# Softmax over rows of 1024: a hand-made critical section handed to the tile framework under a fixed schedule

## The chip, the cores and the metric

The kernel runs on one core of one Trainium2 chip. The metric is the device time of one execution in microseconds (us), the median of several runs.

## The reference, cut to what matters

```python
x: 32 x 512 x 1024 float32, temperature = 0.5
scaled  = x / temperature
shifted = scaled - max(scaled, axis=-1)
out     = exp(shifted) / sum(exp(shifted), axis=-1)
```

That is 16,384 rows of 1024 numbers. 67.11 MB are read and 67.11 MB written.

## The kernel before

The rows are cut into 16 tiles of 4 MB (128 partitions, 8 rows each). SyncE issues the loads, VectorE takes maxima and divides, ScalarE computes exponentials with their sums and issues the stores. Six places of 32 KB per partition form a ring: load i+6 waits until store i has landed. Every tile is worked on in two groups of four rows. All waits are written by hand, inside one critical section, with 37 semaphores: one for each load, one for each store, and five counters.

```python
LOADS = [8] * 16; STORES = [[8]] * 16; RING = 48; GROUP = 4
ring = pool.tile([P, RING, d], f32, name="ring")          # one tensor, six places
...
loaded = [tc.alloc_semaphore(f"loaded{i}") for i in range(len(LOADS))]
stored = [tc.alloc_semaphore(f"stored{i}") for i in range(len(parts))]
topped, biased, summed, inverted, scaled = (tc.alloc_semaphore(name) for name in ...)

def exponential(g):
    i, s, r, k = groups[g]
    nc.scalar.wait_ge(biased, g + 1)
    for a in range(k):
        ins = nc.scalar.activation(ring[:, s + a, :], ring[:, s + a, :], Exp,
              bias=bias[:, r + a : r + a + 1], scale=scale, accum_out=sums[:, r + a : r + a + 1])
    ins.then_inc(summed, 1)

def store(n):
    l, s, r, k = parts[n]
    nc.scalar.wait_ge(scaled, part_end[n])                 # the division of this tile only
    nc.scalar.dma_start(out=dram(of, r, k, l), in_=ring[:, s : s + k, :]).then_inc(stored[n], 16)

with tc.tile_critical():
    for i in range(len(LOADS)):
        load(i)                                            # from load 6 on: waits for stored[i - 6]
    for b in range(free_to + 1, len(parts)):
        nc.sync.wait_ge(stored[b], 16)
    ...                                                    # exponential(g), store(n) on ScalarE
    ...                                                    # maximum, shift, invert, divide on VectorE
```

Of the kernel before, what the change touches and what calls it, by code (L numbers as in the profile page):

```python
# [1 line left out]

# [4 lines left out]



LOADS = [8] * 16  # L10

STORES = [[8]] * 16

RING = 48

GROUP = 4


def _places(loads, ring):
    places, p = [], 0  # L20
    for k in loads:
        if p + k > ring:
            p = 0
        places.append(p)
        p += k
    return places


@with_exitstack
def kernel(  # L30
    ctx: ExitStack,
    tc: tile.TileContext,
    x: bass.AP,
    temperature: bass.AP,
    out: bass.AP,
):
    nc = tc.nc
    f32 = mybir.dt.float32
    scale = 1.0 / float(temperature)
    extreme = mybir.AluOpType.max if scale > 0 else mybir.AluOpType.min  # L40

    P = 128
    xf = x.flatten_outer_dims()
    of = out.flatten_outer_dims()
    n, d = xf.shape
    assert sum(LOADS) * P == n

    places = _places(LOADS, RING)
    first = [sum(LOADS[:i]) for i in range(len(LOADS))]
    total = sum(LOADS)  # L50

    pool = ctx.enter_context(tc.tile_pool(name="data", bufs=1))
    ring = pool.tile([P, RING, d], f32, name="ring")
    top = pool.tile([P, total], f32, name="top")
    bias = pool.tile([P, total], f32, name="bias")
    sums = pool.tile([P, total], f32, name="sums")
    recip = pool.tile([P, total], f32, name="recip")


    parts = []  # L60
    for i, ks in enumerate(STORES):
        j = 0
        for k in ks:
            parts.append((i, places[i] + j, first[i] + j, k))
            j += k
        assert j == LOADS[i]

    groups, part_end = [], []
    for i, s, r, k in parts:
        for a in range(0, k, GROUP):  # L70
            groups.append((i, s + a, r + a, min(GROUP, k - a)))
        part_end.append(len(groups))

    loaded = [tc.alloc_semaphore(f"loaded{i}") for i in range(len(LOADS))]
    stored = [tc.alloc_semaphore(f"stored{i}") for i in range(len(parts))]
    topped, biased, summed, inverted, scaled = (
        tc.alloc_semaphore(name)
        for name in ("topped", "biased", "summed", "inverted", "scaled")
    )

    def dram(t, r, k, i):

        block = t[P * first[i] : P * (first[i] + LOADS[i]), :]
        block = block.rearrange("(p k) d -> p k d", p=P, k=LOADS[i])
        return block[:, r - first[i] : r - first[i] + k, :]

    def maximum(g):
        i, s, r, k = groups[g]
        if g == 0 or groups[g - 1][0] != i:
            nc.vector.wait_ge(loaded[i], 16)  # L90
        nc.vector.tensor_reduce(  # L91
            out=top[:, r : r + k],
            in_=ring[:, s : s + k, :],
            axis=mybir.AxisListType.X,
            op=extreme,
        ).then_inc(topped, 1)

    def shift(g):
        i, s, r, k = groups[g]
        nc.vector.wait_ge(topped, g + 1)  # L100
        nc.vector.tensor_scalar_mul(  # L101
            bias[:, r : r + k], in0=top[:, r : r + k], scalar1=-scale
        ).then_inc(biased, 1)

    def exponential(g):
        i, s, r, k = groups[g]
        nc.scalar.wait_ge(biased, g + 1)
        for a in range(k):
            ins = nc.scalar.activation(  # L109
                ring[:, s + a, :],  # L110
                ring[:, s + a, :],
                mybir.ActivationFunctionType.Exp,
                bias=bias[:, r + a : r + a + 1],
                scale=scale,
                accum_out=sums[:, r + a : r + a + 1],
            )
        ins.then_inc(summed, 1)

    def invert(g):
        i, s, r, k = groups[g]  # L120
        nc.vector.wait_ge(summed, g + 1)
        nc.vector.reciprocal(recip[:, r : r + k], sums[:, r : r + k]).then_inc(inverted, 1)  # L122

    def divide(g):
        i, s, r, k = groups[g]
        nc.vector.wait_ge(inverted, g + 1)
        for a in range(k):
            ins = nc.vector.tensor_scalar_mul(  # L128
                ring[:, s + a, :], in0=ring[:, s + a, :], scalar1=recip[:, r + a : r + a + 1]
            )  # L130
        ins.then_inc(scaled, 1)

    def load(i):
        nonlocal free_to
        s, r, k = places[i], first[i], LOADS[i]

        for n, (l, s1, r1, k1) in enumerate(parts):
            if l < i and s1 < s + k and s < s1 + k1 and n > free_to:
                for b in range(free_to + 1, n + 1):
                    nc.sync.wait_ge(stored[b], 16)  # L140
                free_to = n
        nc.sync.dma_start(out=ring[:, s : s + k, :], in_=dram(xf, r, k, i)).then_inc(
            loaded[i], 16
        )

    def store(n):
        l, s, r, k = parts[n]
        nc.scalar.wait_ge(scaled, part_end[n])
        nc.scalar.dma_start(out=dram(of, r, k, l), in_=ring[:, s : s + k, :]).then_inc(
            stored[n], 16  # L150
        )

    free_to = -1
    with tc.tile_critical():  # L154
        for i in range(len(LOADS)):
            load(i)
        for b in range(free_to + 1, len(parts)):
            nc.sync.wait_ge(stored[b], 16)


        for g in range(len(groups) + 1):
            if g < len(groups):
                exponential(g)
            for n in range(len(parts)):
                if part_end[n] == g:
                    store(n)


        for g in range(len(groups) + 1):
            if g < len(groups):  # L170
                maximum(g)
                shift(g)
            if g > 0:
                invert(g - 1)
                divide(g - 1)


# [1 line left out]
_INS = ['x', 'temperature']  # L179
_OUTS = [((32, 512, 1024), 'float32')]  # L180

_NUMBERS = {'temperature': 0.5}


# [26 lines left out]
```

## Time and profile before

| | before |
|---|---|
| time, median of 6 runs | 318.76 us (318.69 to 318.99) |
| span in the profile | 317.0 us |
| bytes moved | 134.25 MB |
| VectorE, ScalarE busy | 74%, 47% |
| first load issued | 0.94 us |
| last store issued, landed | 302.64, 315.12 us |

Where a landing is given as a point of time, it is the end of the transfer's last packet, unless the text says otherwise. The semaphore that tells of it moves 0.3 to 0.4 us later (at 315.50 us for this store); the profile's times from issue to landing, and all waits, count to that.

First the page of the profile. The rows DMA and GB/s cut the span into 40 equal slices: the busy share of the 16 transfer engines in tenths, and what they moved.

```profile
span 317.0 us, 568 instructions
...
DVE 235.5 (74%) x224; ACT 149.6 (47%) x257; POOL 0.2 (0%) x4
...
DMA  8999999999999999999999999999999999999995
GB/s 323 405 459 409 389 442 418 447 428 442 434 430 438 422 438 426 442 422 442 422 447 430 434 434 430 435 426 438 430 438 435 434 426 434 434 426 434 430 434 232
```

No compute engine is full, but the transfers are, in every slice but the first and last. So the transfers bound the kernel. A load or a store of 4 MB that has the engines to itself takes up 9.68 us of them, which is 433 GB/s (the first three loads land at 13.02, 22.70 and 32.38 us; stores 12 to 14, after the last load, land 9.66 and 9.67 us apart), and the 32 of them come to 309.8 us. Loads and stores together move 432 to 435 GB/s in every stretch between 60 and 300 us.

Next the costliest groups (instruction, shapes, count, busy us, mean ns of one; after the last bar the idle time before it and what ended it) and the transfers (count, KB, median us from issue to landing).

```profile
L109 ACT ACTIVATE ring<-ring,bias 128x1024 f32<-128x1024 f32 x128 | 145.4, 1137 | 149.1 <-DVE bias L101 149.1
L91 DVE TENSOR_REDUCE top<-ring 128x4 f32<-128x4096 f32 x32 | 141.3, 4415 | 62.9 <-DMA ring<-in_x_dram 62.9
...
L109 ACT ACT_TABLE_LOAD x1 | 1.3, 1283 | 0.9 <-SPq L154 0.9
...
ring<-in_x_dram SPq DMA_DIRECT2D x16, 4096.0 KB, 49.9
out_dram<-ring ACTq DMA_DIRECT2D x16, 4096.0 KB, 38.9
```

ScalarE and VectorE have idle time to spare. The time from a store's issue to its landing, 38.9 us, is twice the 19.35 us between two stores; by the times to landing (38.9 and 49.9 us over 19.35) about two stores and two or three loads are under way at any time.

Last, the two ends: first the opening of the chain of waits (start us, length us, what), then the sequencers' instructions of the line that opens and closes the section (count, duration in ns as least/median/most, first and last start); those of the closing line follow in "More of the kernel before".

```profile
0.73 0.06 issue
0.78 0.03 SPq L206
0.82 0.12 issue
0.94 12.41 DMA ring<-in_x_dram
```

```profile
L154 SPq NOP  x2: 13/13/13, 0.7 to 316.0; - x2
L154 SPq EVENT_SEMAPHORE  x2: 17/22/28, 315.7 to 315.9; - x2
L154 SPq COMPARE_BRANCH  x1: 33/33/33, 315.6 to 315.6; - x1
L154 ACTq DRAIN  x1: 8/8/8, 315.8 to 315.8; - x1
L154 DVEq DRAIN  x1: 17/17/17, 315.8 to 315.8; - x1
...
```

```profile
L206 POOLq DRAIN  x3: 34/41/110, 0.7 to 316.7; - x3
...
L206 SPq COMPARE_BRANCH  x1: 33/33/33, 0.8 to 0.8; - x1
L206 POOLq EVENT_SEMAPHORE_RANGE_CLEAR  x1: 265/265/265, 316.4 to 316.4; - x1
```

The reader should see that a section costs a signal and a branch on the way in (0.7 to 0.9 us, before the first load), and a branch, a signal and drains on the way out (315.6 to 316.0 us, after the last store).

### The profile page before, as it was taken

The numbers are of one execution on the slowest core, as the hardware profiler recorded it, in microseconds if no ns is written. First come the engines' busy times: TensorE is split into PE (matmuls) and PEld (weight loads), VectorE is DVE, ScalarE is ACT, GpSimd is POOL, SyncE is SP. The second block draws the span as 40 slices with busy tenths as digits, with TensorE's granted clock in tenths as the row PEclk, the third lists the DMA queues.
The fourth block names the chain that finished last, engine by engine and source line by source line (L and its number), as shares of the span: only waits on it lengthen the run. The fifth ranks groups of instructions, "written<-read, shape, count | busy, mean of one in ns | idle before, by whom it ended". The sixth has DMA issues, their size and how long they took to land.

```text
span 317.0 us, 568 instructions
## 1 busy us (share of the span) xinstructions
DVE 235.5 (74%) x224; ACT 149.6 (47%) x257; POOL 0.2 (0%) x4
## 2 busy tenths in 40 slices
DVE  0399999999689494995949769496793967949710
ACT  1076666666526255361554606455163551635500
POOL 0000000000000000000000000000000000000000
DMA  8999999999999999999999999999999999999995
GB/s 323 405 459 409 389 442 418 447 428 442 434 430 438 422 438 426 442 422 442 422 447 430 434 434 430 435 426 438 430 438 435 434 426 434 434 426 434 430 434 232
DMA packets 4612, 134.25 MB, mean 424 GB/s; under 512 B 512, under 2 KB 512, under 8 KB 512
## 3 DMA queue, kind: packets, MB, share of 16 engines
q1 hardware_dynamic: 2304, 67.11, 49.6%
q10 hardware_dynamic: 2304, 67.11, 49.0%
q14 instruction: 4, 0.03, 0.0%
HBM read 67.11 MB, written 67.11 MB: 423 GB/s over the span
## 4 chain that ended last, share of the span: by engine, by line
DMA 57%; DVE 29%; ACT 5%; another core or an unknown queue 4%; issue 0%; SPq 0%
DMA ring<-in_x_dram 35%; DMA out_dram<-ring 22%; DVE top L91 18%; DVE ring L128 10%; ACT ring L109 5%; DVE bias L101 1%; DVE recip L122 0%; SPq L206 0%; SPq L154 0%
## 5 line engine op out<-in xcount | busy, mean ns | idle before, releaser
L109 ACT ACTIVATE ring<-ring,bias 128x1024 f32<-128x1024 f32 x128 | 145.4, 1137 | 149.1 <-DVE bias L101 149.1
L91 DVE TENSOR_REDUCE top<-ring 128x4 f32<-128x4096 f32 x32 | 141.3, 4415 | 62.9 <-DMA ring<-in_x_dram 62.9
L128 DVE TENSOR_SCALAR ring<-ring,recip 128x1024 f32<-128x1024 f32 x128 | 87.7, 749 | 1.1
L109 ACT ACTIVATION_READ_ACCUMULATOR ring<-ring,bias 128x1 f32 x128 | 23.9, 186 | 0.0
L122 DVE RECIPROCAL recip<-sums 128x4 f32<-128x4 f32 x32 | 5.5, 171 | 2.0 <-ACT ring L109 2.0
L101 DVE TENSOR_SCALAR bias<-top 128x4 f32<-128x4 f32 x32 | 5.4, 170 | 1.1
L109 ACT ACT_TABLE_LOAD x1 | 1.3, 1283 | 0.9 <-SPq L154 0.9
L192 POOL MEMSET const-bfloat16-1.0<- 128x1 bf16 x1 | 0.1, 102 | 0.0
L192 POOL MEMSET const-uint8-127<- 128x1 uint8 x1 | 0.1, 102 | 0.0
L192 POOL MEMSET const-float32-0.0<- 128x1 f32 x1 | 0.1, 99 | 0.2 <-issue 0.2
L192 POOL MEMSET const-float32-1.0<- 128x1 f32 x1 | 0.1, 99 | 0.0
## 6 DMA issues: line engine op xcount, KB each, us to landing
ring<-in_x_dram SPq DMA_DIRECT2D x16, 4096.0 KB, 49.9
out_dram<-ring ACTq DMA_DIRECT2D x16, 4096.0 KB, 38.9
```

The lines of the kernel that those rows point to most:

```text
L91: nc.vector.tensor_reduce(out=top[:, r : r + k], in_=ring[:, s : s + k, :], axis=mybir.AxisListType.X, op=extreme,).then_inc(topped, 1)
L101: nc.vector.tensor_scalar_mul(bias[:, r : r + k], in0=top[:, r : r + k], scalar1=-scale).then_inc(biased, 1)
L109: ins = nc.scalar.activation(ring[:, s + a, :], ring[:, s + a, :], mybir.ActivationFunctionType.Exp, bias=bias[:, r + a : r + a + 1], scal ...
L122: nc.vector.reciprocal(recip[:, r : r + k], sums[:, r : r + k]).then_inc(inverted, 1)
L128: ins = nc.vector.tensor_scalar_mul(ring[:, s + a, :], in0=ring[:, s + a, :], scalar1=recip[:, r + a : r + a + 1])
L192: nc = _bacc.Bacc("TRN2", target_bir_lowering=False, num_devices=1)
```

## The change

The intent is to have the framework do what was written by hand, at no cost. The ring becomes a pool of six tiles, the statistics become small tiles in four rotating buffers, and the framework makes all semaphores. A fixed schedule keeps each engine's instructions in the order they are written, which is the order of before.

```diff
-    ring = pool.tile([P, RING, d], f32, name="ring")
-    loaded = [...]; stored = [...]; topped, biased, summed, inverted, scaled = ...
+    data = ctx.enter_context(tc.tile_pool(name="data", bufs=BUFS))      # BUFS = 6
+    stats = ctx.enter_context(tc.tile_pool(name="stats", bufs=4))
...
+    def load():
+        i = len(tiles)
+        if i < len(TILES):
+            xt = data.tile([P, sum(TILES[i]), d], f32, name="xt")
+            nc.sync.dma_start(out=xt, in_=dram(xf, i))
+            tiles.append(xt)
...                                    # maximum, exponential, divide: the same, without waits
-    with tc.tile_critical():
-        (three loops, one for each engine)
+    with tc.manual_schedule():
+        for _ in range(BUFS):
+            load()
         for g in range(len(groups) + 1):
             if g < len(groups):
                 maximum(g)
-                shift(g)
+                exponential(g)
             if g > 0:
-                invert(g - 1)
                 divide(g - 1)
+                store(g - 1)           # and, after a tile's last store, load()
```

In the built program the order on each engine is the same. The semaphores are not: all 32 transfers share eight, which the framework hands out in turn, so a transfer also waits for the one that had its semaphore before; for the stores that need this wait it is the store three or four back.

More of the change, by code (lines that the diff above doesn't have):

```diff
@@ L6 @@
 from concourse._compat import with_exitstack
-LOADS = [8] * 16
-STORES = [[8]] * 16
-RING = 48
+TILES = [[8]] * 16
+BUFS = 6
 GROUP = 4
-def _places(loads, ring):
-    places, p = [], 0
-    for k in loads:
-        if p + k > ring:
-            p = 0
-        places.append(p)
-        p += k
-    return places
 @with_exitstack
@@ L45 @@
     n, d = xf.shape
-    assert sum(LOADS) * P == n
-    places = _places(LOADS, RING)
-    first = [sum(LOADS[:i]) for i in range(len(LOADS))]
-    total = sum(LOADS)
-    pool = ctx.enter_context(tc.tile_pool(name="data", bufs=1))
-    ring = pool.tile([P, RING, d], f32, name="ring")
-    top = pool.tile([P, total], f32, name="top")
-    bias = pool.tile([P, total], f32, name="bias")
-    sums = pool.tile([P, total], f32, name="sums")
-    recip = pool.tile([P, total], f32, name="recip")
-    parts = []
@@ L61 @@
-    for i, ks in enumerate(STORES):
-        j = 0
-        for k in ks:
-            parts.append((i, places[i] + j, first[i] + j, k))
-            j += k
-        assert j == LOADS[i]
-    groups, part_end = [], []
-    for i, s, r, k in parts:
-        for a in range(0, k, GROUP):
-            groups.append((i, s + a, r + a, min(GROUP, k - a)))
-        part_end.append(len(groups))
-    loaded = [tc.alloc_semaphore(f"loaded{i}") for i in range(len(LOADS))]
-    stored = [tc.alloc_semaphore(f"stored{i}") for i in range(len(parts))]
@@ L76 @@
-    topped, biased, summed, inverted, scaled = (
-        tc.alloc_semaphore(name)
-        for name in ("topped", "biased", "summed", "inverted", "scaled")
-    )
-    def dram(t, r, k, i):
-        block = t[P * first[i] : P * (first[i] + LOADS[i]), :]
-        block = block.rearrange("(p k) d -> p k d", p=P, k=LOADS[i])
-        return block[:, r - first[i] : r - first[i] + k, :]
-    def maximum(g):
-        i, s, r, k = groups[g]
-        if g == 0 or groups[g - 1][0] != i:
-            nc.vector.wait_ge(loaded[i], 16)
-        nc.vector.tensor_reduce(
-            out=top[:, r : r + k],
-            in_=ring[:, s : s + k, :],
-            axis=mybir.AxisListType.X,
-            op=extreme,
-        ).then_inc(topped, 1)
@@ L98, in shift @@
-    def shift(g):
-        i, s, r, k = groups[g]
-        nc.vector.wait_ge(topped, g + 1)
-        nc.vector.tensor_scalar_mul(
-            bias[:, r : r + k], in0=top[:, r : r + k], scalar1=-scale
-        ).then_inc(biased, 1)
-    def exponential(g):
-        i, s, r, k = groups[g]
-        nc.scalar.wait_ge(biased, g + 1)
-        for a in range(k):
-            ins = nc.scalar.activation(
-                ring[:, s + a, :],
-                ring[:, s + a, :],
+    assert sum(sum(ks) for ks in TILES) * P == n
@@ new lines, with dram @@
+    data = ctx.enter_context(tc.tile_pool(name="data", bufs=BUFS))
+    stats = ctx.enter_context(tc.tile_pool(name="stats", bufs=4))
+    groups, first, r = [], [], 0
+    for i, ks in enumerate(TILES):
+        first.append(r)
+        r += sum(ks)
+        a = 0
+        for k in ks:
+            for b in range(0, k, GROUP):
+                m = min(GROUP, k - b)
+                groups.append((i, a + b, m, (a, k) if b + m == k else None))
+            a += k
+    def dram(t, i):
+        k = sum(TILES[i])
+        block = t[P * first[i] : P * (first[i] + k), :]
+        return block.rearrange("(p k) d -> p k d", p=P, k=k)
@@ new lines @@
+    tiles, small = [], []
+    def load():
[4 more added lines that the diff above has]
+            tiles.append(xt)
+    def maximum(g):
+        i, a, k, _ = groups[g]
+        top, bias, sums, recip = (
+            stats.tile([P, k], f32, name=name) for name in ("top", "bias", "sums", "recip")
+        )
+        small.append((bias, sums, recip))
+        nc.vector.tensor_reduce(
+            out=top, in_=tiles[i][:, a : a + k, :], axis=mybir.AxisListType.X, op=extreme
+        )
+        nc.vector.tensor_scalar_mul(bias, in0=top, scalar1=-scale)
@@ L112, in exponential @@
+    def exponential(g):
+        i, a, k, _ = groups[g]
+        bias, sums, _ = small[g]
+        for b in range(k):
+            nc.scalar.activation(
+                tiles[i][:, a + b, :],
+                tiles[i][:, a + b, :],
                 mybir.ActivationFunctionType.Exp,
-                bias=bias[:, r + a : r + a + 1],
+                bias=bias[:, b : b + 1],
                 scale=scale,
-                accum_out=sums[:, r + a : r + a + 1],
+                accum_out=sums[:, b : b + 1],
@@ L116, in exponential @@
             )
-        ins.then_inc(summed, 1)
-    def invert(g):
-        i, s, r, k = groups[g]
-        nc.vector.wait_ge(summed, g + 1)
-        nc.vector.reciprocal(recip[:, r : r + k], sums[:, r : r + k]).then_inc(inverted, 1)
-    def divide(g):
-        i, s, r, k = groups[g]
-        nc.vector.wait_ge(inverted, g + 1)
-        for a in range(k):
-            ins = nc.vector.tensor_scalar_mul(
-                ring[:, s + a, :], in0=ring[:, s + a, :], scalar1=recip[:, r + a : r + a + 1]
-            )
-        ins.then_inc(scaled, 1)
@@ L133, in load @@
-    def load(i):
-        nonlocal free_to
-        s, r, k = places[i], first[i], LOADS[i]
-        for n, (l, s1, r1, k1) in enumerate(parts):
-            if l < i and s1 < s + k and s < s1 + k1 and n > free_to:
-                for b in range(free_to + 1, n + 1):
-                    nc.sync.wait_ge(stored[b], 16)
-                free_to = n
-        nc.sync.dma_start(out=ring[:, s : s + k, :], in_=dram(xf, r, k, i)).then_inc(
-            loaded[i], 16
-        )
-    def store(n):
-        l, s, r, k = parts[n]
-        nc.scalar.wait_ge(scaled, part_end[n])
-        nc.scalar.dma_start(out=dram(of, r, k, l), in_=ring[:, s : s + k, :]).then_inc(
-            stored[n], 16
-        )
@@ L153 @@
-    free_to = -1
-    with tc.tile_critical():
-        for i in range(len(LOADS)):
-            load(i)
-        for b in range(free_to + 1, len(parts)):
-            nc.sync.wait_ge(stored[b], 16)
-        for g in range(len(groups) + 1):
-            if g < len(groups):
-                exponential(g)
-            for n in range(len(parts)):
-                if part_end[n] == g:
-                    store(n)
+    def divide(g):
+        i, a, k, _ = groups[g]
+        _, sums, recip = small[g]
+        nc.vector.reciprocal(recip, sums)
+        for b in range(k):
+            nc.vector.tensor_scalar_mul(
+                tiles[i][:, a + b, :], in0=tiles[i][:, a + b, :], scalar1=recip[:, b : b + 1]
+            )
@@ L169, with store @@
+    def store(g):
+        i, _, _, part = groups[g]
+        if part:
+            a, k = part
+            nc.scalar.dma_start(out=dram(of, i)[:, a : a + k, :], in_=tiles[i][:, a : a + k, :])
+            if a + k == sum(TILES[i]):
+                load()
+    with tc.manual_schedule():
+        for _ in range(BUFS):
+            load()
         for g in range(len(groups) + 1):
```

## The prediction

> **What bounds the kernel now.** The transfers. The profile's slice table shows the DMA engines at 9 tenths or more in every slice but the first and last, and the table by stage gives a DMA share of 1.00 and 432 to 435 GB/s between 60 and 300 us. The page counts 134.25 MB moved; at 433 GB/s that is 310 us of the 317.0 us span (an estimate from these two). The rest is a start before the engines are full (first slice 323 GB/s) and an end (last slice 232 GB/s): the last store is issued at 302.6 us and takes 12.9 us, which leaves 1.5 us for the closing handshakes. VectorE is busy 74%, ScalarE 47%; VectorE waits 62.9 us for loads. [...]
>
> **What the change does.** The built instructions stand in the same order on VectorE, ScalarE and SyncE: 16 loads of 4 MB from SyncE, 16 stores from ScalarE, 128 exponentials, 32 maxima (4415 ns each), 128 divisions. No byte and no elementwise work is added or removed. Six pooled tiles are the same six places of the ring, freed by the same stores. What differs:
> 1. Removed: the branch into and out of the critical section. At the start three engines pass one more semaphore and branch before the first load (0.94 us); at the end SyncE's release, drains and another branch. I estimate 0.1 to 0.2 us at each end, from the pieces of the chain of waits between 0.67 and 0.94 us and from the 1.5 us tail. All of it is on the critical path.
> 2. Added: about 45 separate semaphore waits on ScalarE, for double conditions; [...] on an engine that idles 149 us. A store waits for the division, which ends some 2.7 us later, so no store is delayed.
> 3. Added: transfers share eight semaphores, so a store also waits for the store three or four before it. Store 4 (about 92 us) waits for store 1, which landed at 77 us; later a store takes 39 us and the waited-for one was issued 77 us earlier (period 19.35 us). Never late.
> 4. Moved: the exponential table load (1.28 us) now waits for the first load, at 13.4 us. The first exponential starts at 18.0 us, after maximum and bias, so it stays hidden.
> 5. Moved: statistics in four rotating buffers; their reuse waits for work four groups old. Tiles 1 to 5 lie in reverse address order, which I expect to mean nothing.
>
> **Predicted time.** 318.73 - 0.3 = 318.4 us, range 317.6 to 319.5. Chances: faster by over 2% 0.01, within 2% 0.97, slower by over 2% 0.02.
>
> **What would show it.** The same DMA share and GB/s; times to landing still near 49.9 and 38.9 us (medians); VectorE's wait for loads near 63 us; first load 0.1 to 0.2 us earlier; the tail after the last landing a little under 1.5 us; table load at 13.4 us, first exponential still at about 17.9 us; ScalarE idle within 3 us of before.
>
> **What would make it wrong.** A shared semaphore that blocks ScalarE's queue after all, seen as a store issued more than 0.1 us after its last division; a load waiting for a later store than the one whose place it takes; closing waits that cost more than the removed branches (then up to 0.5 us slower); an address layout that lowers the 433 GB/s.

Two passages are cut from it, marked where they stood: a comparison of the 433 GB/s with figures that no run of this case shows, and a length for each added wait that does not say which numbers it comes from. 318.73 us less 0.3 us for the two ends of the section gives the 318.4 us.

## The result, and the profile after

| | before | after |
|---|---|---|
| time, median of 6 runs | 318.76 us (318.69 to 318.99) | 317.95 us (317.86 to 318.30) |
| ratio | | 0.9975, 95% interval 0.9962 to 0.9987 |
| span in the profile | 317.0 us | 316.0 us |

Ratios here are the mean time of one kernel's runs over that of the other's runs of the same rounds, so they are not quite the ratio of the medians quoted. Executions over 1.5% slower than the fastest of the same kernel are left out of the means.

The page and the groups of the changed kernel:

```profile
span 316.0 us, 620 instructions
...
DVE 235.5 (75%) x224; ACT 149.6 (47%) x257; POOL 0.2 (0%) x4
...
DMA  8999999999999999999999999999999999999996
GB/s 332 411 452 423 373 460 415 452 425 431 436 427 440 427 444 423 444 419 448 415 452 411 452 408 456 423 444 427 436 431 432 440 423 444 419 444 419 452 411 274
```

```profile
L79 ACT ACTIVATE xt<-xt,bias 128x1024 f32<-128x1024 f32 x128 | 145.4, 1137 | 136.8 <-DVE recip L91 119.4
L70 DVE TENSOR_REDUCE top<-xt 128x4 f32<-128x4096 f32 x32 | 141.3, 4416 | 62.6 <-DMA xt<-in_x_dram 62.6
...
L79 ACT ACT_TABLE_LOAD x1 | 1.3, 1283 | 13.0 <-DMA xt<-in_x_dram 13.0
...
xt<-in_x_dram SPq DMA_DIRECT2D x16, 4096.0 KB, 50.2
out_dram<-xt ACTq DMA_DIRECT2D x16, 4096.0 KB, 38.6
```

Hardly anything in the body has moved: the same busy times, the same durations, 62.6 us of waiting for loads against 62.9, and times to landing within 0.3 us of before. ScalarE's idle time is 136.8 + 13.0 = 149.8 us, before it was 149.1 + 0.9 = 150.0 us; the table load has only moved inside it. (The exponentials' wait now carries the name of the reciprocal, since the profile names the last of the events that a combined wait could have been ended by; it is the same wait.)

The two ends of the changed kernel, in the same three views:

```profile
0.66 0.07 issue
0.73 12.21 DMA xt<-in_x_dram
```

```profile
L147 SPq EVENT_SEMAPHORE  x7: 17/28/28, 270.5 to 315.9; - x7
L147 POOLq EVENT_SEMAPHORE  x4: 17/17/17, 315.4 to 315.9; - x4
L147 POOLq DRAIN  x3: 34/41/70, 0.7 to 315.7; - x3
...
L147 POOLq EVENT_SEMAPHORE_RANGE_CLEAR  x1: 92/92/92, 315.6 to 315.6; - x1
```

No branch and no drain of a section is left, and the clear has shrunk from 265 to 92 ns. The start and end times of the sequencers' records in the two traces give this account of the 1.00 us between the two spans:

| stretch | before us | after us | saved us |
|---|---|---|---|
| start to first load's issue | 0.937 | 0.730 | 0.207 |
| first load's issue to last store's landing (the body) | 314.187 | 314.073 | 0.114 |
| landing to the start of the clear | 1.310 | 0.806 | 0.504 |
| the clear | 0.265 | 0.092 | 0.173 |
| end of the clear to the end | 0.291 | 0.291 | 0.000 |

The ends account for 0.88 us, at least the 0.81 us by which the medians differ. But this is one pair of traces. The experiments ask whether the ends really cost that much, and whether anything in the body helps or harms.

### The profile page after: what moved, and what is told of

Same layout as the page of the kernel before. It is cut to its first block, busy times and chain, and to the rows that moved or that the text cites. A ratio compares the mean times of both kernels' runs of the same rounds, so it can differ in the third digit from the quotient of the medians.

```text
span 316.0 us, 620 instructions
## 1 busy us (share of the span) xinstructions
DVE 235.5 (75%) x224; ACT 149.6 (47%) x257; POOL 0.2 (0%) x4
## 4 chain that ended last, share of the span: by engine, by line
DVE 49%; DMA 32%; another core or an unknown queue 9%; ACT 5%; issue 1%; DVEq 0%; SPq 0%
DVE top L70 29%; DMA xt<-in_x_dram 20%; DVE xt L93 18%; DMA out_dram<-xt 12%; ACT xt L79 5%; DVE recip L91 1%; DVE bias L73 1%; DVEq L147 0%; SPq L61 0%
## 5 line engine op out<-in xcount | busy, mean ns | idle before, releaser
L79 ACT ACTIVATE xt<-xt,bias 128x1024 f32<-128x1024 f32 x128 | 145.4, 1137 | 136.8 <-DVE recip L91 119.4
L70 DVE TENSOR_REDUCE top<-xt 128x4 f32<-128x4096 f32 x32 | 141.3, 4416 | 62.6 <-DMA xt<-in_x_dram 62.6
L93 DVE TENSOR_SCALAR xt<-xt,recip 128x1024 f32<-128x1024 f32 x128 | 87.7, 749 | 1.1
L79 ACT ACTIVATION_READ_ACCUMULATOR xt<-xt,bias 128x1 f32 x128 | 23.9, 187 | 0.0
```

Of the source, the lines that this page charges most:

```text
L70: nc.vector.tensor_reduce(out=top, in_=tiles[i][:, a : a + k, :], axis=mybir.AxisListType.X, op=extreme)
L79: nc.scalar.activation(tiles[i][:, a + b, :], tiles[i][:, a + b, :], mybir.ActivationFunctionType.Exp, bias=bias[:, b : b + 1], scale=scal ...
L93: nc.vector.tensor_scalar_mul(tiles[i][:, a + b, :], in0=tiles[i][:, a + b, :], scalar1=recip[:, b : b + 1])
```

## The experiments

Theory 1: the gain sits at the two ends (the section's entry and exit, and the clear), and the body is the same because the transfers bound it. Theory 2, the rival: the pool, its address order or its shared semaphores change the body by a few tenths of a us, and the ends cost little.

### 124 spare semaphores in the changed kernel

```diff
     tiles, small = [], []
+    spare = [tc.alloc_semaphore(f"spare{i}") for i in range(124)]
```

> The changed kernel with 124 semaphores allocated and never used. Theory 1 (the gain sits at the two ends of the program; part of it is that fewer semaphores are cleared at the end: 10 instead of 41, 92 ns instead of 265 ns in the two traces, so 5.6 ns for each): the clear grows to 36 + 134 x 5.6 = 784 ns, the time by 0.69 us to about 318.6 us, and everything before the clear stays as in the changed kernel. Theory 2 (the gain lies in the body: pooled tiles or shared semaphores make the transfers faster, the clear does not depend on the number): the clear stays near 92 ns and the time at 317.95 us.

It took 318.81 us (5 runs; before, in the same rounds, 318.87; ratio 0.9999, interval 0.9985 to 1.0013). The sequencers' instructions of the closing line:

```profile
L148 POOLq DRAIN  x3: 34/41/245, 0.7 to 316.4; - x3
...
L148 POOLq EVENT_SEMAPHORE_RANGE_CLEAR  x1: 764/764/764, 315.6 to 315.6; - x1
```

The clear grew from 92 to 764 ns for 124 semaphores, so 5.4 ns for each. The drain just before it grew too, from 70 to 245 ns, so 1.4 ns for each; I had not expected that. The first load was still issued at 0.73 us. The clear still began at 315.6 us, but only because the last store happened to land 0.12 us sooner. The time rose by 0.86 us over the changed kernel's 317.95, and the clear and its drain explain 0.85 of it. Semaphores that are never used cost time at the end, and enough of them undo the gain.

### Fewer semaphores in the kernel before

```diff
-    loaded = [tc.alloc_semaphore(f"loaded{i}") for i in range(len(LOADS))]
-    stored = [tc.alloc_semaphore(f"stored{i}") for i in range(len(parts))]
+    loaded = [tc.alloc_semaphore(f"loaded{i}") for i in range(8)]
+    stored = [tc.alloc_semaphore(f"stored{i}") for i in range(8)]
     ...   # number i becomes i % 8, the awaited count 16 * (i // 8 + 1)
```

> The kernel before with 8 rotating load semaphores and 8 rotating store semaphores in place of 16 and 16, so 25 are cleared instead of 41. Theory 1: the clear takes 36 + 25 x 5.6 = 176 ns instead of 265, so 0.09 us less, 318.65 us; first load at 0.94 us and a tail of about 1.4 us as before. Theory 2 (sharing semaphores between transfers is what helps the body): half or more of the 0.8 us gain, 318.3 us or less, with the last store landing earlier.

It took 318.85 us (ratio 0.9997, interval 0.9985 to 1.0010), and the clear of 25 semaphores took 178 ns:

```profile
L206 POOLq EVENT_SEMAPHORE_RANGE_CLEAR  x1: 178/178/178, 316.6 to 316.6; - x1
```

Four points (10, 25, 41 and 134 semaphores; 92, 178, 265 and 764 ns) thus lie close to one line, and so do the drains before the clear (70, 93, 110 and 245 ns). The saving of 0.1 us is too small for the times to show, and sharing semaphores brought nothing else: the body took 314.36 us against 314.19.

### A critical section put back at the end, and its control

The control writes one element per partition of the last tile after its store has landed. The second kernel makes the same write inside a critical section.

```diff
+    nc.vector.memset(tiles[-1][:, 0, 0:1], 0.0)               # control
```

```diff
+    with tc.tile_critical():                                  # with a section
+        nc.sync.nop()
+        nc.scalar.nop()
+        nc.vector.memset(tiles[-1][:, 0, 0:1], 0.0)
```

> The changed kernel with one write of one element per partition into the last tile, after its store has landed: the control for the next run. It adds a short VectorE instruction and one hop to the end. Both theories: 0.05 to 0.2 us over the changed kernel, 318.0 to 318.2 us.

> The same write, inside an otherwise empty critical section at the end, so that the section's way in and way out are paid after the last store has landed. Theory 1 (leaving the section costs 0.46 us at the end): 0.45 to 0.7 us over the control without a section, about 318.6 to 318.8 us, with the same clear of about 95 ns. Theory 2: within 0.1 us of the control.

The control took 317.98 us (ratio to before 0.9978), the kernel with the section 318.88 us (1.0002): 0.90 us more, all of the gain and a little over. In the traces the tail from the last landing to the end is 1.30 us in the control and 2.26 us with the section. The branches are back; the clear is hardly longer:

```profile
L151 DVEq COMPARE_BRANCH  x1: 53/53/53, 315.5 to 315.5; - x1
L151 SPq COMPARE_BRANCH  x1: 33/33/33, 315.7 to 315.7; - x1
L151 ACTq COMPARE_BRANCH  x1: 41/41/41, 315.7 to 315.7; - x1
L151 POOLq EVENT_SEMAPHORE_RANGE_CLEAR  x1: 114/114/114, 316.7 to 316.7; - x1
```

This is more than the 0.45 to 0.7 us that I expected, because I had put down the exit alone. Here the entry is paid at the end too, with waits for shared semaphores: in the trace SyncE has ten semaphore instructions on the closing line, against seven in the control, and five more on the section's own line. In the kernel before, the entry costs 0.21 us at the start, and from the last landing to the clear 0.50 us more pass than in the changed kernel, of which 0.04 is the longer drain of more semaphores. That leaves 0.67 us for the section, against 0.90 for the whole section at the end.

### The pool's address order in the kernel before

```diff
-    places = _places(LOADS, RING)
+    places = [-p % RING for p in _places(LOADS, RING)]
```

> The kernel before with the ring's places taken in the pool's address order (0, then 40 down to 8). Theory 1 (the body is bound by transfers that don't care where the six places lie): unchanged, 318.8 us, with 313.9 to 314.4 us from the first load's issue to the last store's landing. Theory 2 (the pool's address order helps the transfers): half or more of the 0.8 us, 318.4 us or less, all of it between these two points.

It took 318.75 us (before, in the same rounds, 318.72; ratio 1.0001, interval 0.9989 to 1.0014). The body took 314.37 us. The address order does nothing.

### The late table load in the kernel before

```diff
+    if g == 0:
+        nc.scalar.wait_ge(loaded[0], 16)
     nc.scalar.wait_ge(biased, g + 1)
```

> The kernel before with one more wait on ScalarE, so that the table of the exponential is loaded only after the first tile, as in the changed kernel. Theory 1: hidden; the first exponential still starts 0.2 us after the first bias, at 18.0 us, and the time stays at 318.8 us. Rival (the early table load at 0.9 us slows the first load, which took 12.41 us before and 12.21 after): the first load lands 0.2 us earlier, 318.6 us. If the table load is put after the wait for the bias instead, the first exponential comes 1.3 us later, but the transfers stay saturated and the time moves by less than 0.5 us.

It took 318.67 us (ratio 0.9997, interval 0.9981 to 1.0012). As I had feared, the table was loaded after the wait for the bias, at 17.9 us, so the first exponential came at 19.17 instead of 18.03 us and the first store at 34.22 instead of 33.07 us. The last store still landed at 315.10 us (315.12 before). So even a real delay of 1.15 us at the first store is swallowed: the page of this run still has the transfer engines at 9 tenths in every slice but the first and last, since loads are queued meanwhile (in the kernel before six are issued by 3.42 us, and the sixth lands at 86.8). This is the plainest evidence that the body does not care about small delays on ScalarE. The first load's shorter way to landing does not come from the table load either: from issue to landing it took 12.08 us before and 11.86 after, but also 11.86 here, 11.81 with the reversed places and 12.05 with the spare semaphores. That is scatter.

### A wait for an earlier store, at distance one and two

The prediction said that the shared semaphores cost nothing because the awaited store has long landed. If so, it is the distance that matters. Two kernels put such a wait into the kernel before, with transfers of 4 MB as they were.

```diff
     nc.scalar.wait_ge(scaled, part_end[n])
+    if n >= 1:                                # distance two: n >= 2, stored[n - 2]
+        nc.scalar.wait_ge(stored[n - 1], 16)
```

> The kernel before, with each store also made to wait until the store just before it has landed; transfers of 4 MB as they were. Theory 1 (the framework's wait for a store three or four back costs nothing because stores are issued every 19.35 us and land after 39 us, so a wait three back has 19 us of slack, and a wait one back is short by 20 us): stores are issued up to 20 us after their last division, first store 1 at 57.5 instead of 47.9 us, and ScalarE's exponentials behind them are held. The time rises, by 1 to 10 us; the rise is small if the transfer engines stay full with loads. Rival (such a wait is free at any distance): 318.8 us and stores within 0.1 us of their division.

> The same with the wait two stores back, at the edge: 38.7 us between the two issues against 39 us from issue to landing. Theory 1: store 2 (62.6 us) is not held, since store 0 has landed at 57.5 us; in the steady state stores are held by about 0.3 to 1 us; time within 1 us of 318.8 us. Rival: no hold at all, 318.8 us.

At distance two the time was 318.82 us (before, in the same rounds, 318.96; ratio 0.9998). At distance one it was 354.35 us (352.80 to 356.12; ratio 1.1113, interval 1.1066 to 1.1160): 35 us slower. Waits on ScalarE (for what; total us, times, longest us), and GB/s and transfers from the page, of the kernel at distance one:

```profile
ACT ring L109 <- DMA out_dram<-ring: 151.1, 11, 16.7
```

```profile
GB/s 322 444 418 425 403 437 437 427 418 425 436 440 411 440 274 363 462 240 459 370 326 444 263 448 414 296 414 296 415 429 281 414 297 414 355 355 296 348 303 296
...
ring<-in_x_dram SPq DMA_DIRECT2D x16, 4096.0 KB, 23.1
out_dram<-ring ACTq DMA_DIRECT2D x16, 4096.0 KB, 22.6
```

Stores 1 to 11 were issued 10 to 18 us after their last division, and the exponentials behind them waited 151 us. I had expected 1 to 10 us, with the engines kept full by loads. They were not: a load needs a place that a store frees, so with one store in flight there was soon one load in flight as well (23.1 us to landing instead of 49.9), and the rate fell to 240 to 300 GB/s in every second or third slice. Stores came 22.6 us apart instead of 19.35. In the profiled run the last store landed 37.4 us later than before (352.5 against 315.1). Of these the last load accounts for 8.8 us (291.2 against 282.4), and the other 28.6 us came after it, since five stores were still to be issued, one after another, where before it was two. The last three stores were not held themselves; they came some 12 to 15 us apart, with their divisions. At distance two no store was held at all: all were issued within 0.04 us of their last division, which came at least 0.25 us after the awaited landing (by the semaphores: store 5 landed at 153.91 us, the last division of tile 7 ended at 154.17). I had expected to see holds of 0.3 to 1 us. In the trace of before store 5 had landed 0.7 us too late for that; why the landings came slightly earlier in this run is not settled.

So the changed kernel, whose awaited stores lie three and four back, has one to two periods of 19.35 us to spare. Its own trace shows the same from the other side. These are ScalarE's separate waits ahead of stores, first in the changed kernel, then in the kernel at distance one:

```profile
L101 ACTq EVENT_SEMAPHORE  x5: 17/17/17, 93.1 to 209.7; - x5
```

```profile
L150 ACTq EVENT_SEMAPHORE  x15: 17/17/17, 57.8 to 340.7; - x15
```

The 17 ns prove nothing: at distance one, where stores were held for 10 to 18 us, the records are as short, because they start only when the wait is over (the first at 57.77 us, just after the semaphore of store 0 at 57.75). The times of start prove it. In the changed kernel the five waits ran at 93.06, 151.08, 170.44, 190.36 and 209.70 us, which is 16 to 36 us after the awaited store had landed and 2.5 us before the end of the tile's last division. All 16 stores were issued 0.03 to 0.04 us after that division, as in the kernel before.

### More transfers over the same eight semaphores

Loads in four pieces of 1 MB, in both kernels:

```diff
-    nc.sync.dma_start(out=xt, in_=dram(xf, i))
+    for q in range(0, 8, 2):
+        nc.sync.dma_start(out=xt[:, q : q + 2, :], in_=dram(xf, i)[:, q : q + 2, :])
```

> The kernel before with each 4 MB load given as four loads of 1 MB, all counted on the tile's own semaphore: the control for the next run. Both theories: the same bytes in the same order, so within 1 us of 318.8 us; stores still issued within 0.1 us of their last division.

> The changed kernel with each load given as four loads of 1 MB, so that 80 transfers go round the eight shared semaphores and nearly every store must wait for the store just before it (in the changed kernel: three or four stores before it). Theory 1 (the shared semaphores cost nothing in the changed kernel only because the store waited for has long landed): store 1, ready at about 47.5 us, is held until store 0 lands, about 9 us later, ScalarE's exponentials behind it are held too, and only one store is in flight at a time; at least 2 us slower than the control, perhaps 3 to 10. Rival (a shared semaphore is no restraint worth speaking of, whatever its distance): within 1 us of the changed kernel, 318 us.

The control failed. With its own semaphore for each tile, the kernel before took 333.99 us in pieces (330.93 to 334.57, ratio 1.0459), and the changed kernel 329.39 us (ratio 1.0320). Both are slower than before, and the one with the shared semaphores is the faster of the two, where I had expected it to be the slower by 2 us or more. The control's queues (packets, MB, share of the engines' time; q1 holds the loads, q10 the stores) and its transfers:

```profile
q1 hardware_dynamic: 9216, 67.11, 49.2%
q10 hardware_dynamic: 2304, 67.11, 47.4%
...
ring<-in_x_dram SPq DMA_DIRECT2D x64, 1024.0 KB, 46.9
out_dram<-ring ACTq DMA_DIRECT2D x16, 4096.0 KB, 16.5
```

A store now lands after 16.5 us instead of 38.9. The same bytes go in four times as many packets on the loads' queue: in the trace a load's packet has 8 KB (309 ns, median), since a piece holds two rows of each partition, while a store's packet has 32 KB (1213 ns). How the engines choose between two queues that both have work was not shown; the shares are measured: from 4 to 11 us after the issue of stores 1 to 12, the stores moved 354 GB/s and the loads 77, a ratio of 4.6 with packets of four times the size, where in the same stretches of the kernel before it is 1.4 with equal packets (249 against 184 GB/s). So the loads starve, and at the end the engines stand half empty (195 to 255 GB/s in two of the last five slices of this run). The shared semaphores of the changed kernel held stores back, by up to 22 us, and its loads as well. Why it is still the faster of the two is not settled; its loads did not gain, since the last of them landed at 302.9 us against 291.5 in the control. That unequal packets cause the loss was tested by cutting the stores in the same way, so that both queues have packets of 8 KB:

```diff
-    nc.scalar.dma_start(out=dram(of, ...), in_=...)           # one store of 4 MB
+    for q in range(0, 8, 2):
+        nc.scalar.dma_start(out=dram(of, ...)[:, q : q + 2, :], in_=...[:, q : q + 2, :])
```

> The kernel before with loads and stores both given as four transfers of 1 MB, so that the packets of both queues are 8 KB. Theory P (the 15 us that four loads of 1 MB cost came from unequal packets: 8 KB against 32 KB[...], so stores landed after 16.5 us and loads starved): with equal packets stores land again after about 39 us and the loads' shortage at the end goes; the time is 318.8 us plus some 2% for the smaller packets (309 ns against a quarter of 1213 ns), 322 to 327 us. Rival (the number of load transfers costs it): 333 us or more, with stores still landing after less than 20 us.

> The changed kernel with loads and stores both given as four transfers of 1 MB: 128 transfers over eight shared semaphores, so each piece waits for the piece eight before it, about one tile back. Theory 1: the pieces of a store are held back well over 1 us after their last division and at most eight transfers are in flight; slower than the control with its own semaphores for each tile by 1 to 10 us. Rival: 0.8 us faster than that control, as the changed kernel is against the kernel before.

With equal packets the control took 322.60 us (322.48 to 322.77, ratio 1.0116), and its rate was 424 to 429 GB/s in nearly every slice:

```profile
GB/s 292 425 425 421 401 428 426 428 425 429 426 428 427 428 426 429 428 428 427 427 427 428 427 429 426 427 428 428 428 429 424 426 428 429 428 428 427 426 428 246
...
out_dram<-ring ACTq DMA_DIRECT2D x64, 1024.0 KB, 28.3
```

Of the 15 us that the pieces had cost, 11 went when the packets were made equal (333.99 to 322.60). The 3.6 us that remain are 1.2%, not quite the 1.9% by which four packets of 8 KB (4 x 309 ns) take longer than one of 32 KB (1213 ns). The stores got their share back: a tile's store again took 39 to 40 us from the first piece's issue to the last one's landing, and stores and loads moved 213 and 214 GB/s, a ratio of 0.99. So the shares moved with the packet sizes, and this speaks against the rival that the number of load transfers costs the time.

And now the shared semaphores show their cost: the changed kernel with 128 pieces took 330.09 us (329.97 to 331.71), 2.3% more than its control (330.09 over 322.60). The last piece of a tile's store was issued 7 to 22 us after its last division for the tiles 1 to 11, against 1.4 to 2.9 us in the control, and ScalarE's exponentials stood behind it. The loads waited too, for earlier loads with the same semaphore, which they do not in the control (who waited for what; total us, times, longest us):

```profile
ACT xt L80 <- DMA out_dram<-xt: 35.5, 3, 14.4
```

```profile
SPq L62 <- DMA xt<-in_x_dram: 113.2, 23, 12.1
SPq L62 <- DMA out_dram<-xt: 110.9, 12, 24.1
```

So the same handing-out of semaphores that is free with 32 transfers goes with a loss of 7.5 us with 128. The two kernels differ by the whole change, and no run gives the pooled kernel semaphores of its own, so the parts of held stores and held loads in the 7.5 us are not shown.

## Why the prediction was right

The time was right (317.95 us, predicted 318.4, range 317.6 to 319.5), and so was the reason: the transfers bound both kernels, and only the ends could move. The gain was 0.8 us where I had put 0.3; the range held it, the sum behind it was too small. Point by point:

- **What bounds the kernel.** Right. The transfer engines are full in both traces. The body took 314.07 us after and 314.19 before, and 313.95 to 314.46 in the seven other profiled kernels that move whole tiles with no store held (spare, few, both end kernels, reversed, late table, distance two). A body effect of 0.1 to 0.2 us is neither shown nor excluded; the ends alone cover the gain.
- **Point 1, the section removed.** Right in kind, too small in size; this is the term that was mis-sized. I put 0.1 to 0.2 us at each end, 0.3 us in all. The start saved 0.207 us. The end saved 0.504 us up to the clear (0.46 without the shorter drain), more than twice the estimate, since the exit is not one branch but a row of hand-overs: release, three drains, a signal back, another wait, and only then the closing barrier. In the trace of before the row takes 0.46 us of SyncE, from 315.585 to 316.043 us. The branch alone takes 155 ns to the start of the next instruction (315.740 us), though its record shows 33 ns; the plain wait just before it takes 65 ns from start to start. "The tail after the last landing a little under 1.5 us" was wrong in the same way: from SyncE's last wait to the end it went from 1.47 to 0.80 us.
- **A term I did not list.** The clear of the semaphores saved 0.173 us, and the drain before it 0.040. I had counted the semaphores only for what they wait for, not for their being reset. The semaphore experiments give 5.4 ns for each in the clear and 1.4 ns in the drain.
- **Point 2, added waits on ScalarE.** Right. There are 40 of them in the trace. 26 of their records are 17 ns long; the other 14, which wait for two semaphores, are 4.6 to 7.4 us long. Two that follow each other start 55 ns apart (107.473 and 107.528 us), and no store moved.
- **Point 3, shared semaphores never late.** Right, and shown from both sides: in the trace the waits were over 16 to 36 us after the landing they were for, with no store held; no cost at distance two, 35 us at distance one.
- **Point 4, the table load.** Right. It moved to 13.0 us, and the first exponential started at 17.63 us, 0.2 us after the start of the bias, as before. (I said 17.9; the first load landed 0.2 us sooner than its earlier issue explains, which the other runs show to be scatter.)
- **Point 5, address order.** Right: 318.75 us with the places reversed.

No version beat the changed kernel. The 32 transfers need 309.8 us of the 316.0 even at the 9.68 us that one takes alone, and the experiments that touched the body only lost.

## What to carry to other kernels

When the transfers bound a kernel and the order of work stays the same, handing hand-made waits to the framework can cost nothing, as here with 32 transfers, and removing a critical section saves something at the ends: here 0.67 us (no kernel of another length was run). Count also the semaphores, here 6.8 ns each with the drain. Before sharing semaphores between transfers, work out how far back the awaited transfer lies, and compare that distance times the period with the time from issue to landing: two periods were enough here, one cost 11%. And keep the packets of two competing queues the same size, since cutting only the loads gave the engines to the stores (354 GB/s against 77) and cost 4.6%.
